# A recurrence filled at a lower pace, two jobs swapped, and two heads' queries copied out of their banks

## The chip, the cores and the metric

The kernel runs on one core of one Trainium2 chip. The metric is the device time of one execution, in microseconds; the time before is the median of three runs. The engines are TensorE (PE), VectorE (DVE), ScalarE (ACT) and GpSimd (POOL); SyncE (SP) issues most of the loads. Each engine works through its instructions in order and waits on semaphores for the others.

## The reference

One layer of a streaming encoder, on 1024 tokens of width 1024 in float32. Two branches read the same normalised input: stick-breaking attention with 8 heads of 64, and an HGRN2 recurrence with 4 heads of 128. Sigmoid gates merge them, an MLP of width 4096 follows.

```python
xn = rmsnorm(x, norm1_g[layer])
u = xn @ w_in[layer]
q_sb, k_sb, v_sb, f_raw, i_hg, q_hg, g_hg, gate_sb, gate_hg = jnp.split(u, c, axis=-1)
o_sb = merge_heads(stick_breaking_attention(q_sb, k_sb, v_sb))      # by blocks of 128 queries
f = lb + (1.0 - lb) * sigmoid(f_raw)
k_hg = (1.0 - lb) * sigmoid(-f_raw)
# S_t = diag(f_t) S_{t-1} + k_t v_t^T ;  o_t = S_t^T q_t
o_hg = hgrn2_chunkwise(silu(q_hg), k_hg, i_hg, log(f))
o_hg = merge_heads(rmsnorm(o_hg, hg_norm_g)) * silu(g_hg)
g_a, g_b = sigmoid(gate_sb + bg[:D]), sigmoid(gate_hg + bg[D:])
merged = g_a * (o_sb @ w_o_sb) + g_b * (o_hg @ w_o_hg)
h = x + merged @ w_out
h = h + square(relu(rmsnorm(h, norm2_g) @ w_ff1)) @ w_ff2
return rmsnorm(h, final_g)
```

## The kernel before, in words

All products are made in float32 precision from three products of a high and a low half: `three` issues hi·hi, hi·lo and lo·hi, each a 128x128 weight tile against 128x512 moving columns. A weight is split into its halves by a cast on ACT and a subtraction on DVE (`hi_lo`, L156 and L161).

The program has these stages: the first norm, transposes and projections; the attention (about 50 to 330 us), in which items of one head and query block go through `scores`, `weights`, `turn` and `values`; the recurrence (about 330 to 583 us), head by head; the gate products (`gates`, tiles gX, gY); the output projection; the MLP.

The attention and the recurrence are chains over PE, ACT, DVE and POOL which would leave PE waiting. So a stream of jobs, `st`, runs beside them: the projections of the attention's later heads (qk), of the recurrence's forget gates (f0 to f3), queries (q0 to q3) and values (i), ten raw products for the gates (raw0 to raw9; raw8 and raw9 are the two sums for the recurrence's output gates; their tiles are pga8 and pga9, pgq8 and pgq9) and the attention's output projection (sb0 to sb3, tiles pys0 to pys7). A step of a job is six products. `Stream.step` starts a job by splitting its weights and, by `prefetch`, splits the weights of the next job and loads those of the one after. In the attention, `st.advance` takes a share of the steps after each item, up to the job `j_att`, which `st.finish(j_att)` completes at the attention's end.

In the recurrence a pass of the loop over h works at two generators in turn: the levels of head h (`hg_levels`: eight levels of shorter and shorter spans; each multiplies k and q by the decay pp on DVE, and PE makes the scores sl or sd from them, copied out under a mask), and the tail of head h−1 (`hg_tail`: pk, the transposes of k; pkv, the products of k and v; the updates of the state on DVE, L1172; pho0 and pho1, the outputs of the two halves; their norm hon over ACT, POOL and DVE; and pot0 and pot1, its transposes). So the last head's tail is alone in the pass h=4. At each yield of either generator `FILL[h]` steps of the stream are owed, and the whole ones are taken, up to a job that is set for each pass:

```python
upto = (j_i, j_raw[1], j_raw[6], j_sb[1], j_sb[2])[h]
...
owed += FILL[h]
st.advance(int(owed), upto)
owed -= int(owed)
```

A side generator, `sum_forms`, makes the sums of the input for the gate products (tiles gs, L1236 and L1239, with their halves gsh and gsl) from the accumulated inputs that four accumulate-DMAs of POOL write into xnl; one step of it goes with each step of an sb job. Its first sum needs the accumulate-DMAs that raw7 issues (`whole_input`).

What PE, DVE and the others execute is fixed when the program is built: a scheduler puts the instructions of each engine into one order, by the order of the code and its own estimates. The edits therefore move more than the lines they touch.

In the stream the job q_h ends with `silu_epilogue`: ACT takes the sigmoid of a PSUM bank (tile pjq), and DVE multiplies the bank by it; the bank is free for another tile after that.

Of the kernel before, what the change touches and what calls it, by code (L numbers as in the profile page):

```python
# [23 lines left out]
KT = D // P  # L24
# [15 lines left out]
def kernel(  # L40
# [19 lines left out]
    nc = tc.nc  # L60
# [14 lines left out]
    def slot(name, dt=F32):  # L75
        return spool.tile([P, 1024], dt, tag="s", name=name)

    def slot_n(name, n, dt=F32):

        if n <= 512:  # L80
            return hpool.tile([P, 512], dt, tag="h", name=name)
        return slot(name, dt)

    def bank(name):
        return psum.tile([P, 512], F32, tag="p", name=name)
# [49 lines left out]
    def load(dst, src):  # L135
        last_load[0] = after(nc.sync.dma_start(dst, src), last_load[0])
# [4 lines left out]
    def lo_now(behind=None):  # L141
        while owed_wlo:
            after(owed_wlo.pop()(), behind)
# [24 lines left out]
    def mul(out, a, b):  # L168
        return nc.vector.tensor_tensor(out=out, in0=a, in1=b, op=ALU.mult)  # L169
# [317 lines left out]
    class Stream:  # L487
# [8 lines left out]
        def add(self, units, body):  # L496
            self.jobs.append((units, body))
            return len(self.jobs)

        def _start(self):  # L500
            lo_now()
            units, body = self.jobs[self.pos]
            for u in units:
                u.split()
            if (self.pos > 0 or self.eager) and not units[-1].late:
                self.prefetch()
            self.gen = body()

# [44 lines left out]
    def three(ps, wh, wl, xh, xl, first, last, goes_on=False):  # L553
        matmul(ps, wh, xh, start=first, stop=False, skip_group_check=goes_on)
        matmul(ps, wh, xl, start=False, stop=False, skip_group_check=goes_on)
        matmul(ps, wl, xh, start=False, stop=last, skip_group_check=goes_on)
# [37 lines left out]
    def wide_unit(name, mat, c0, n):  # L594
        rows = 1024 // n * P
        return Unit(
            name,
            [
                [(0, n, mat[r : r + rows, c0 : c0 + n].rearrange("(k p) c -> p k c", p=P))]
                for r in range(0, D, rows)  # L600
            ],
            wide=True,
        )
# [298 lines left out]
    def hg_slot(h, key, half):  # L902
        if half == 0:
            hg[h, key] = slot(f"{key}{h}")
        return hg[h, key][:, half * 512 : (half + 1) * 512]
# [28 lines left out]
    u_i = wide_unit("wi", W_IN, C_I, HGW)  # L934
# [18 lines left out]
    def silu_epilogue(h, key):  # L953
        def ep(ps, half):
            t = hg_slot(h, key, half)
            nc.scalar.activation(t, ps, AF.Sigmoid)
            mul(t, ps, t)

        return ep

    j_f, j_q = {}, {}

    def f_job(h):
        u = cols_unit(f"wf{h}", [(W_IN, C_F + h * P, P)])
        j_f[h] = proj_jobs([(f"pjf{h}", u, f_epilogue(h))], xn)

    def q_job(h):
        u = cols_unit(f"wq{h}", [(W_IN, C_QH + h * P, P)])
        j_q[h] = proj_jobs([(f"pjq{h}", u, silu_epilogue(h, "q"))], xn)
# [262 lines left out]
    def half(name, dt=F32):  # L1232
        return hpool.tile([P, 512], dt, tag="h", name=name)
# [36 lines left out]
    def gate_bias(which, cb):  # L1270
        return prm[:, BG + which * KT + cb : BG + which * KT + cb + 1]
# [44 lines left out]
    def raw_job(cb):  # L1316
        u = raw_units[cb]

        def steps_of(ps, wt, w0, half_, k0, start):
            wh, wl = u.hl[wt]  # L1320
            for k in range(4):
                c = (w0 + k) * P
                xh, xl = xn.mov(k0 + k, half_)
                three(
                    ps, wh[:, c : c + P], wl[:, c : c + P], xh, xl, start and k == 0, k == 3, True
                )
                if k % 2 == 1:
                    yield

        def body():  # L1330
            p1, p14, g1 = (half(f"{n}_{cb}") for n in ("p1", "p14", "g1"))
            ps, p4 = bank(f"pga{cb}"), bank(f"pgq{cb}")
            if 6 <= cb < KT:
                load_g1(cb - 6)
            if 5 <= cb < KT:
                sb_units[cb - 5].load()
            if 3 <= cb < KT - 1:
                osb[cb - 3] = slot(f"osr{cb}")
                load(osb[cb - 3], od[cb - 3])
            yield from steps_of(ps, 0, 0, 0, 0, True)  # L1340
            hi_behind[0] = nc.scalar.copy(p1, ps)
            nc.scalar.dma_start(pd[cb][:, 0, :], p1)
            u.split_t()
            st.prefetch()
            hi_behind[0] = None
            yield from steps_of(p4, 1, 0, 1, 4, True)
            add(p14, p1, p4)
            if cb == 3 or cb == KT - 1:
                whole_input(1, int(cb == KT - 1))
            nc.gpsimd.dma_start(pd[cb][:, 1, :], p14)  # L1350
            yield from steps_of(ps, 0, 4, 0, 4, False)
            if cb < KT:
                nc.scalar.activation(g1, ps, AF.Sigmoid, bias=gate_bias(0, cb))
            else:
                nc.scalar.activation(g1, ps, AF.Sigmoid)
                mul(g1, ps, g1)
            nc.scalar.dma_start(gd[cb], g1)
            if 4 <= cb < KT:
                a_sb.put(cb - 4, osb.pop(cb - 4))

        return st.add([u], body)
# [3 lines left out]
    def load_g1(cb):  # L1365
        g1r[cb] = half(f"g1r{cb}")
        load(g1r[cb], gd[cb])
# [4 lines left out]
    def whole_input(i, j):  # L1372
        for kp in range(2):
            h, l = (t.bitcast(F32) for t in xn.t[i, 2 * j + kp])
            nc.gpsimd.dma_start(l, h, accum_op=ALU.add)
            whole[i, j, kp] = l
# [82 lines left out]
    f_job(0)  # L1459
    f_job(1)  # L1460
    q_job(1)
    raw_job(KT + 1)
    f_job(2)
    j_att = j_f[2]
    q_job(2)
    j_i = i_job()
    f_job(3)
# [858 lines left out]
        values(*ready.popleft())  # L2326


    FILL = (3.4, 2.2, 2.8, 2.9, 2.9)
    owed = 0.0  # L2330
    for h in range(NHG + 1):
        lev = hg_levels(h) if h < NHG else iter(())
# [3 lines left out]
        while going:  # L2336
            going = False
            for g in (lev, tail):
# [3 lines left out]
                if next(g, StopIteration) is not StopIteration:  # L2342
                    going = True
                    owed += FILL[h]
                    st.advance(int(owed), upto)
# [105 lines left out]
```

## Time and profile before

| what | us |
|---|---|
| median of three runs | 1451.55 (1451.54 to 1451.67) |
| the profiled execution | 1451.45 |
| its span | 1449.7 |
| PE busy | 1429.0 |
| DVE busy | 1118.8 |
| ACT busy | 676.5 |
| POOL busy | 142.5 |

The mean granted clock of TensorE was 0.995. A row of PE's waits reads: the tile that PE wanted to write, the engine and tile that it waited for, and total us, times, longest. A row of the timeline reads: start, duration, engine, line, operation, output and inputs, shape, and in brackets the idle time ahead of it with what ended it. Matmuls are pipelined, so a 128x512 product shows 0.39 us and starts 0.23 us after the one before it. A helper has one line for all its uses (L128 is every product, L161 and L169 most subtractions and multiplications on DVE), so the tile's name tells the place.

### The profile page before, as it was taken

The numbers are of one execution on the slowest core, as the hardware profiler recorded it, in microseconds if no ns is written. First come the engines' busy times: TensorE is split into PE (matmuls) and PEld (weight loads), VectorE is DVE, ScalarE is ACT, GpSimd is POOL, SyncE is SP. The second block draws the span as 40 slices with busy tenths as digits, with TensorE's granted clock in tenths as the row PEclk, the third lists the DMA queues.
The fourth block names the chain that finished last, engine by engine and source line by source line (L and its number), as shares of the span: only waits on it lengthen the run. The fifth ranks groups of instructions, "written<-read, shape, count | busy, mean of one in ns | idle before, by whom it ended". The sixth has DMA issues, their size and how long they took to land.

```text
span 1449.7 us, 19206 instructions
## 1 busy us (share of the span) xinstructions
PE 1429.0 (99%) x7056; PEld 1197.9 (83%) x7056; DVE 1118.8 (77%) x1537; ACT 676.5 (47%) x1173; POOL 142.5 (10%) x338
## 2 busy tenths in 40 slices
PE   9999999999999998999999999999999999999998
PEld 8888888888888887788888888888888888888886
DVE  6579999999568889588877898666666757768765
ACT  6366666673233434333235574444444533423443
POOL 3022222110011031000000200000000000000032
PEclk9999999999999999899999999999999999999999
DMA  7123445453025774355488414444445974676825
GB/s 235 28 66 88 117 101 89 75 108 117 0 61 155 234 202 164 117 166 176 132 293 278 146 59 141 151 159 155 150 160 191 352 262 182 246 277 246 281 101 184
DMA packets 161333, 233.53 MB, mean 161 GB/s; under 512 B 26028, under 2 KB 93144, under 8 KB 161240
## 3 DMA queue, kind: packets, MB, share of 16 engines
q1 hardware_dynamic: 145400, 190.11, 39.1%
q0 software_dynamic: 11520, 34.61, 9.5%
q10 hardware_dynamic: 4320, 7.60, 1.4%
q8 instruction: 55, 0.90, 0.3%
q14 instruction: 38, 0.31, 0.1%
HBM read 167.27 MB, written 65.01 MB: 160 GB/s over the span
## 4 chain that ended last, share of the span: by engine, by line
PE 94%; DVE 3%; ACT 1%; issue 1%; POOL 1%; DMA 0%; ACTq 0%; DVEq 0%; POOLq 0%
PE pm L128 21%; PE pX L128 9%; PE pW L128 6%; PE pY L128 6%; PE pjqk L128 5%; PE gX L128 4%; PE pga L128 4%; PE gY L128 4%; PE pyh L128 3%; PE pys L128 3%; PE pjf L128 3%; PE pjv L128 3%; PE po L128 2%; PE z L128 2%; PE pjq L128 2%; PE pji L128 2%
## 5 line engine op out<-in xcount | busy, mean ns | idle before, releaser
L156 ACT CAST whid<-w 128x1024 fp32r<-128x1024 f32 x30 | 31.6, 1053 | 154.7 <-PE pm L128 86.1
L808 DVE TENSOR_TENSOR_SCAN rm<-rm,bits 128x511 f32<-128x511 f32 (+7 forms) x72 | 87.2, 1218 | 9.0 <-ACT rm L786 8.6
L128 PE MATMUL pm<-wlod,sh 128*128 128x512 f32 x240 | 93.6, 390 | 0.0
L128 PE MATMUL pm<-whid,sl 128*128 128x512 f32 x240 | 93.5, 390 | 0.0
L128 PE MATMUL pm<-whid,sh 128*128 128x512 f32 x240 | 93.5, 389 | 0.0
L128 PE MATMUL pm<-th,sl 128*128 128x512 f32 (+1 forms) x210 | 81.4, 387 | 0.0
L128 PE MATMUL pm<-tl,sh 128*128 128x512 f32 (+1 forms) x210 | 81.4, 387 | 0.0
L128 PE MATMUL pm<-th,sh 128*128 128x512 f32 (+1 forms) x210 | 81.3, 387 | 0.0
L161 DVE TENSOR_TENSOR wlod<-w,whid 128x1024 fp32r<-128x1024 f32 x30 | 36.7, 1223 | 53.3 <-ACT whid L156 53.3
L161 DVE TENSOR_TENSOR sl<-sa,sh 128x1024 fp32r<-128x1024 f32 x56 | 68.3, 1220 | 0.0
L156 ACT CAST wTh<-pw 128x512 fp32r<-128x512 f32 (+2 forms) x96 | 43.4, 485 | 43.1 <-PE pw L131 33.7
L156 ACT CAST sh<-sa 128x1024 fp32r<-128x1024 f32 x56 | 57.2, 1046 | 7.1 <-DMA sa<-ad 7.1
L2087 POOL TENSOR_SCALAR fss<-fss 128x1 f32<-128x1 f32 x8 | 4.5, 561 | 562.1 <-ACT fsc L2082 561.6
L161 DVE TENSOR_TENSOR wTl<-pw,wTh 128x512 fp32r<-128x512 f32 (+2 forms) x96 | 50.2, 546 | 5.6 <-ACT wTh L156 5.3
L128 PEld LDWEIGHTS pm<-wlod,sh 128*128 128x128 f32 x240 | 45.1, 188 | 9.9 <-DVE wlod L161 0.4
L128 PEld LDWEIGHTS pm<-whid,sh 128*128 128x128 f32 x240 | 45.1, 188 | 9.4
L128 PEld LDWEIGHTS pm<-whid,sl 128*128 128x128 f32 x240 | 45.0, 188 | 9.2
L169 DVE TENSOR_TENSOR bt<-bt,rm 128x511 f32<-128x511 f32 (+7 forms) x72 | 49.0, 686 | 3.8
L789 ACT ACTIVATE bt<-z 128x512 f32<-128x512 f32 (+3 forms) x96 | 47.9, 501 | 4.9 <-DMA od<-osb 2.6
L128 PE MATMUL pX<-sql,t1h 128*128 128x512 f32 x128 | 50.1, 391 | 0.1
L128 PE MATMUL pX<-sqh,t1h 128*128 128x512 f32 x128 | 49.9, 390 | 0.0
L128 PE MATMUL pX<-sqh,t1l 128*128 128x512 f32 x128 | 49.9, 390 | 0.0
(931 smaller groups left out, 4473.7 us busy)
## 6 DMA issues: line engine op xcount, KB each, us to landing
w<-in_w_ff_dram SPq DMA_DIRECT2D x72, 512.0 KB, 6.1
sa<-ad SPq DMA_DIRECT2D x56, 512.0 KB, 7.1
ad<-a SPq DMA_DIRECT2D x32, 256.0 KB, 2.2
ad<-s SPq DMA_DIRECT2D x16, 512.0 KB, 5.5
tw<-in_w_out_dram POOLq DMA_DIRECT2D x24, 256.0 KB, 4.1
pr<-pd SPq DMA_DIRECT2D x10, 512.0 KB, 5.1
x<-in_x_dram SPq DMA_DIRECT2D x8, 512.0 KB, 9.7
xnl<-xnh POOLq DMA_DIRECT2D x8, 512.0 KB, 9.4
```

Source lines behind the costliest of these rows:

```text
L128: return pe(nc.tensor.matmul(*a, **k))
L156: hi_last[0] = after(in_turn("act", nc.scalar.copy(dst, src)), hi_behind[0])
L161: nc.vector.tensor_tensor(out=dst, in0=src, in1=hi.bitcast(F32), op=ALU.subtract),
L169: return nc.vector.tensor_tensor(out=out, in0=a, in1=b, op=ALU.mult)
L789: nc.scalar.activation(bt[:, s0 : s0 + e], z[:, :e], AF.Sigmoid, scale=0.125)
L808: sc = nc.vector.tensor_tensor_scan(out=rr, data0=rr, data1=bits[:, 1024 - nk + a : 1024 - nk + b][:, ::-1], initial=rm[:, b : b + 1] if i ...
L2087: nc.gpsimd.tensor_scalar(out=ssq, in0=ssq, scalar1=1.0 / D, scalar2=EPS, op0=ALU.mult, op1=ALU.add)
```

## The change

```diff
@@ class Stream, _start @@
             units, body = self.jobs[self.pos]
             for u in units:
                 u.split()
-            if (self.pos > 0 or self.eager) and not units[-1].late:
+            if (self.pos > 0 or self.eager) and not units[-1].late and units[-1] is not u_i:
                 self.prefetch()
             self.gen = body()
@@ silu_epilogue @@
             t = hg_slot(h, key, half)
             nc.scalar.activation(t, ps, AF.Sigmoid)
+            if h < 2:
+                x = slot_n(f"qx{h}_{half}", 512)
+                nc.scalar.copy(x, ps)
+                ps = x
             mul(t, ps, t)
@@ the stream's jobs @@
     f_job(0)
     f_job(1)
     q_job(1)
-    raw_job(KT + 1)
     f_job(2)
-    j_att = j_f[2]
+    j_att = raw_job(KT + 1)
     q_job(2)
@@ the recurrence @@
-    FILL = (3.4, 2.2, 2.8, 2.9, 2.9)
+    FILL = (3.4, 2.0, 2.6, 2.6, 2.9)
```

There are four edits. The pace of the passes h=1, 2 and 3 is 2.0, 2.6 and 2.6 steps for each yield, where it was 2.2, 2.8 and 2.9. The job raw9 comes behind f2, and is the last that the attention completes. When the job i starts, the weights of the next job, f3, aren't split yet, and those of q3 aren't loaded. For q of heads 0 and 1, ACT copies the bank (two halves each) into an SBUF tile qx, and DVE multiplies from there.

On PE, at the end of the recurrence, before the change. The rows are the last of the second half's output pho of head 3, the two transposes pot, and the first gate product gX.

```order
L128 MATMUL pho_1_5876<-v_3976,sc_5170 128x128
L128 MATMUL pho_1_5876<-k_4436,q_4559 128x128
L131 MATMUL pot_0_5895<-ident,hon_0_5842 128x128 x4
L131 MATMUL pot_1_5901<-ident,hon_1_5878 128x128 x4
L128 MATMUL gX_5907<-gsh_5634,whig_5765 128x512
```

And with the change, from the last of the eighteen fill products (pys4 and pys5) that stand behind pho1:

```order
L128 MATMUL pys_0_5872<-asbh_5483,wo02l_5611 128x512
L131 MATMUL pot_0_5885<-ident,hon_0_5764 128x128 x4
L128 MATMUL pys_1_5893<-asbh_5147,wo02h_5610 128x512
L128 MATMUL pys_1_5893<-asbl_5148,wo02h_5610 128x512
L128 MATMUL pys_1_5893<-asbh_5147,wo02l_5611 128x512
...
L128 MATMUL pys_1_5893<-asbh_5483,wo02l_5611 128x512
L131 MATMUL pot_1_5909<-ident,hon_1_5839 128x128 x4
L128 MATMUL gX_5915<-gsh_5697,whig_5807 128x512
```

Twelve fill products (three are shown, and the last) now stand between the two pots, where nothing stood; likewise eighteen between pho1 and pot0.

On DVE, in the levels of the last head, before. The rows begin with the masked copy of level 3's scores; gs are the first sums of the inputs, g1r is the gate of the sb jobs, and the k and q of 128x32x16 are those of level 5.

```order
L1133 COPY_PREDICATED sc_5170<-masks,sl_3_1_5517 128x512
L169 TENSOR_TENSOR g1r_5348<-pys_0_5505,g1r_5348 128x512
L1236 TENSOR_TENSOR gs_5574<-xnl_539,xnl_571 128x1024
L161 TENSOR_TENSOR wo02l_5560<-wo02r_5350,wo02h_5559 128x1024
L161 TENSOR_TENSOR gsl_5583<-gs_5548,gsh_5582 128x1024
L1133 COPY_PREDICATED sc_5170<-masks,sl_4_0_5586 128x512
L169 TENSOR_TENSOR g1r_5503<-pys_0_5567,g1r_5503 128x512
L169 TENSOR_TENSOR k_4436<-k_4436,pp_4435 128x32x16
L169 TENSOR_TENSOR q_4559<-q_4559,pp_4435 128x32x16
```

And with the change, from the same masked copy:

```order
L1137 COPY_PREDICATED sc_5116<-masks,sl_3_1_5455 128x512
L161 TENSOR_TENSOR wo01l_5494<-wo01r_5273,wo01h_5493 128x1024
L1240 TENSOR_TENSOR gs_5605<-xnl_523,xnl_555 128x1024
L169 TENSOR_TENSOR g1r_5271<-pys_0_5497,g1r_5271 128x512
L1137 COPY_PREDICATED sc_5116<-masks,sl_4_0_5514 128x512
L169 TENSOR_TENSOR k_4462<-k_4462,pp_4461 128x32x16
L169 TENSOR_TENSOR q_4573<-q_4573,pp_4461 128x32x16
```

The first sum gs now stands between the masked copy of level 3 and the k and q of level 5, where the second sum, the weights of the third sb job and a half gsl stood.

On DVE, in the first head's levels, before: the subtractions that split the weights of f3 (wf3l) and of q3 (wq3l), and the k and q of levels 3 (128x128x4) and 4 (128x64x8).

```order
L161 TENSOR_TENSOR wf3l_3917<-wf3r_3778,wf3h_3916 128x1024
L169 TENSOR_TENSOR k_2800<-k_2800,pp_2799 128x128x4
L169 TENSOR_TENSOR q_1747<-q_1747,pp_2799 128x128x4
...
L161 TENSOR_TENSOR wq3l_4365<-wq3r_3920,wq3h_4364 128x1024
L1133 COPY_PREDICATED sc_3801<-masks,sl_2_0_3941 128x512
L1133 COPY_PREDICATED sc_3801<-masks,sl_2_1_3946 128x512
L169 TENSOR_TENSOR k_2800<-k_2800,pp_2799 128x64x8
L169 TENSOR_TENSOR q_1747<-q_1747,pp_2799 128x64x8
```

And with the change:

```order
L169 TENSOR_TENSOR k_2804<-k_2804,pp_2803 128x128x4
L169 TENSOR_TENSOR q_1747<-q_1747,pp_2803 128x128x4
...
L161 TENSOR_TENSOR wf3l_4383<-wf3r_3786,wf3h_4382 128x1024
L1137 COPY_PREDICATED sc_3809<-masks,sl_2_0_3943 128x512
L1137 COPY_PREDICATED sc_3809<-masks,sl_2_1_3948 128x512
L169 TENSOR_TENSOR k_2804<-k_2804,pp_2803 128x64x8
L169 TENSOR_TENSOR q_1747<-q_1747,pp_2803 128x64x8
...
L169 TENSOR_TENSOR q_1747<-q_1747,pp_2803 128x32x16
...
L161 TENSOR_TENSOR wq3l_4389<-wq3r_4386,wq3h_4388 128x1024
```

The split of f3's weights stands one level later, that of q3's behind level 5's k and q.

## The prediction

> **What bounds the kernel now.** I read the page's head first, then PE's waits, then the stretch of the recurrence in windows, then the rows of PE and DVE in it.
>
> ```profile
> span 1449.7 us, 19206 instructions
> PE 1429.0 (99%) x7056; PEld 1197.9 (83%) x7056; DVE 1118.8 (77%) x1537; ACT 676.5 (47%) x1173; POOL 142.5 (10%) x338
> ```
>
> PE is busy for 1429.0 of 1449.7 us, and the change adds and removes no matmul. So only the 20.7 us in which PE stands still, and time in which its clock is low, can be won; anything beyond that can only be lost. PE's waits, with total us, times and longest:
>
> ```profile
> PE pot L131 <- DVE hon L169: 2.5, 1, 2.5
> PE pho L128 <- DVE k L1172: 2.3, 3, 1.2
> PE pk L131 <- DVE k L169: 2.0, 1, 2.0
> PE pga L128 <- DVE q L169: 1.3, 1, 1.3
> PE pw L131 <- DVE bt L169: 1.0, 1, 1.0
> PE sl L128 <- DVE q L169: 0.9, 2, 0.7
> ```
>
> Three of them, 6.8 us, lie at the end of the last head's recurrence, and all have DVE behind them. The windows show how that place differs from what is before it (busy us of PE, PEld, DVE, ACT, POOL, then granted clock, DMA share, GB/s):
>
> ```profile
> 495.00:555.00 60.00, 59.85 (x344) 50.84 (x342) 51.98 (x75) 26.00 (x50) 13.27 (x17) 1.00 0.73 211
> 555.00:574.00 19.00, 16.45 (x101) 14.09 (x101) 18.81 (x26) 10.47 (x22) 1.71 (x4) 1.00 0.33 109
> 574.00:584.00 10.00, 5.57 (x24) 4.43 (x25) 6.79 (x11) 5.00 (x13) 2.09 (x3) 0.69 0.33 109
> ```
>
> From 495 to 555 PE hardly waits and DVE has 8.0 us of 60 to spare; from 555 to 574 DVE has 0.2 of 19 to spare and PE loses 2.5; from 574 to 584 PE loses 4.4 of 10. The fill work was spent too early: it covered levels that had room, and the tail, a chain over DVE, ACT and POOL, stands bare. The rows of PE there, and then the chain of waits:
>
> ```profile
> 555.11 1.12 PE L128 MATMUL sl<-q,k 128*64 128x64 f32 x16 [0.26 <-DVE q L169]
> 558.24 0.98 PE L131 MATMUL pk<-ident,k 128*128 128x128 f32 x7 [2.02 <-DVE k L169]
> ...
> 577.64 0.56 PE L128 MATMUL pho<-v,sc 128*128 128x128 f32 x2
> ...
> 582.36 1.12 PE L131 MATMUL pot<-ident,hon 128*128 128x128 f32 x4 [2.54 <-DVE hon L169]
> 583.13 0.78 PE L128 MATMUL gX<-gsh,whig 128*128 128x512 f32 x1
> 583.70 0.63 PE L128 MATMUL gX<-gsl,whig 128*128 128x512 f32 x1
> ...
> 587.97 0.39 PE L128 MATMUL gX<-gsh,wlog 128*128 128x512 f32 x1
> 588.20 0.39 PE L128 MATMUL gY<-gsh,tgh 128*128 128x512 f32 x1
> ```
>
> ```profile
> 579.07 0.82 ACT hon L1195 x6
> 580.57 1.02 POOL hn_y L257
> ...
> 582.36 1.12 PE pot L131 x4
> 583.48 4.88 PE gX L128 x12
> 588.36 2.75 PE gY L128 x12
> ```
>
> A second loss hides in "busy": gX's 12 products take 588.20 − 583.13 = 5.07 us where gY's twelve take 2.75. The granted clock is halved from about 577.7 (the pho row of 0.56 us where its like take 0.39) to 588.0. That costs 2.3 us in gX and some 0.3 in the last pot: 2.6 us.
>
> The row comes first here: the clock fell though no single idle before it was over 1.2 us; PE was about half busy from 574 to 577.7. [...]
>
> **The change, part by part.**
>
> *Pace 2.2, 2.8, 2.9 to 2.0, 2.6, 2.6 for passes 1, 2 and 3.* By the order of the instructions on PE, the count of fill products ahead of each marker falls by 6 at pass 1, by 12 to 24 through pass 2, by 36 at the second head's last levels, by 48 up to level 5 of the last head, and is back at 0 at gX. Nothing is lost: 48 products of 0.23 us (2.75 for twelve), 11 us, move behind. In the tail there now stand eighteen between sl of level 6 and pk where there was none, twelve between pk and pkv, twelve between pkv and pho, eighteen before the second pho, eighteen before the first pot and twelve between the pots. What goes:
> - pk's 2.02: its k comes three wide DVE operations and a narrow one after level 6's q, 4.1 us by the DVE rows below; PE has sl of level 6 (1.12) and eighteen products (4.1) between, 5.2. Gone, with 1.1 us over.
> - pho's 2.3 (three waits on the state updates): eighteen products, 4.1 us, run ahead of the second pho, while DVE does the updates with wide operations between them. Gone, by walking both queues with 0.75 us over at the first pho and 1.5 at the second.
> - pot's 2.54: thirty products, 6.9 us, between the second pho and the last pot, against the 4.7 us from 577.64 to 582.36 in which ACT, POOL and DVE work today. Gone, even with one more wide operation ahead of hon on DVE.
> - sl's 0.26 is counted below. Sum 6.86 us.
> - With PE full, the half clock goes: 2.6 us. If it stays, that stays.
>
> What is late next: PE comes to the levels of the last head up to 11 us sooner. DVE must keep up there:
>
> ```profile
> 551.41 1.22 DVE L161 TENSOR_TENSOR gsl<-gs,gsh 128x1024 fp32r<-128x1024 f32 x1
> 552.54 1.22 DVE L1239 TENSOR_TENSOR gs<-gs,xnl 128x1024 f32<-128x1024 f32 x1
> 553.68 0.69 DVE L169 TENSOR_TENSOR k<-k,pp 128x512 f32<-128x512 f32 x1
> 554.28 0.69 DVE L169 TENSOR_TENSOR q<-q,pp 128x512 f32<-128x512 f32 x1
> ```
>
> From start to start a 1024-wide operation costs 1.13 us, a 512-wide one 0.60. In the new order, between level 5's q and level 6's q, DVE has four wide ones (gs, gsl, gsl, gs), one masked copy and three narrow ones: 4.52 + 0.62 + 1.8 + 0.1 = 7.06 us. PE has sl of level 5 and twelve products between, 1.14 + 2.75 = 3.9, and walking both orders from the end of head 2's tail on, with these durations, puts PE's arrival at level 5 2.3 us behind its q. 7.06 − 3.9 − 2.3 = 0.9 us: PE waits there, where it waited 0.26. The bounds: 0, if the arrival is 0.9 later, and 2.9, the 11 us asked for less the 8.0 that DVE has to spare. I take 0.9, since it follows the order.
>
> A new queueing stands in that walk: gs of the first sum form now waits on DVE ahead of g1r and of level 5's k and q. It needs an accumulate-DMA of POOL; the page's list of DMA issues gives their median, the rows of the tile their spread:
>
> ```profile
> xnl<-xnh POOLq DMA_DIRECT2D x8, 512.0 KB, 9.4
> ```
>
> ```profile
> DMA to landing us min/median/max: 4.6/9.4/13.1
> ```
>
> With a landing near the median the k and q it holds back are still 2.3 us ahead of PE; at 13.1 PE waits about 0.4. From there each us of landing is a us of PE.
>
> *No prefetch at the start of the i job.* The split of wf3 moves from ahead of level 3's k and q to ahead of level 4's, and that of wq3 from ahead of level 4's to after level 5's.
>
> ```profile
> 349.34 1.27 DVE L161 TENSOR_TENSOR wf3l<-wf3r,wf3h 128x1024 fp32r<-128x1024 f32 x1
> ...
> 354.84 1.26 DVE L161 TENSOR_TENSOR wq3l<-wq3r,wq3h 128x1024 fp32r<-128x1024 f32 x1
> ...
> 358.67 2.02 PE L128 MATMUL sl<-q,k 128*128 128x128 f32 x16 [0.67 <-DVE q L169]
> ```
>
> The second one delayed level 4's pair by 1.13 us, and PE waited 0.67 for it: 0.7 us gone. Both splits stay far ahead of the f3 and q3 jobs, which start after all of this head's levels; were wq3 late, f3's products cover it.
>
> *Four copies by ScalarE for q of heads 0 and 1.* No work is saved:
>
> ```profile
> L169 DVE TENSOR_TENSOR q<-q,pp x36: 683/687/693, 334.5 to 558.1; 128x512 f32<-128x512 f32 x36
> L169 DVE TENSOR_TENSOR q<-pjq,q x8: 667/686/693, 156.6 to 435.6; 128x512 f32<-128x512 f32 x8
> ...
> L1341 ACT COPY p<-pga x10: 581/587/622, 169.9 to 518.2; 128x512 f32<-128x512 f32 x10
> ```
>
> The product costs DVE 0.69 us from the bank or from SBUF, and ACT gains four copies of 0.59. [...] What a copy can win is the bank. The first raw job waits 1.26 us for it:
>
> ```profile
> 162.40 1.48 DVE L808 TENSOR_TENSOR_SCAN rm<-rm,bits 128x639 f32<-128x639 f32 x1
> 164.01 0.83 DVE L169 TENSOR_TENSOR bt<-bt,rm 128x639 f32<-128x639 f32 x1
> 164.75 0.69 DVE L169 TENSOR_TENSOR q<-pjq,q 128x512 f32<-128x512 f32 x1
> ```
>
> But the new order puts that 1.48 us scan ahead of the bt that the next pw transposes, and pga behind a wTl on DVE. So pga would still start near 165.5, the wait now standing before pw. Value 0; ends a gain of 1.3 and a loss of 0.6, one copy in line. ACT is 47% busy and hides the rest.
>
> *The tenth raw job behind f2.* It swaps two jobs within the attention. Its add on DVE now comes near the last pair's bt, on which pw waits 0.96 (in the list above); on SP one load of wf2 passes those of the tenth raw job, on POOL one store of p comes later. Nobody reads these for hundreds of us. Value 0, ends ±0.6, one narrow DVE operation.
>
> Sum: −6.86 − 2.6 − 0.67 − 0.26 + 0.9 = −9.5. The profiled execution took 1451.45 us, 0.1 under the median, so 1442.0 us. Some 0.2%, 2.9 us, is what a measurement here can tell from no change.
>
> **The rivals.**
>
> *The waits move in part.* DVE's reserve of 8.0 us is not usable at the levels that need it: DVE must follow PE within one level. Then 2.9 us of waits appear in the last head, and a half-empty stretch brings the low clock back for one spell of the price seen, 2.6. Gain 9.5 − 2.0 − 2.6 = 4.9: 1446.5. For it speaks DVE's 99% from 555 to 574; against it that DVE idled 8.0 us before 555. [...]
>
> *Nothing comes of it*, since the tail is bound by DVE alone: its end would stay at 582.3 whatever PE does, PE only waiting earlier. 1451.5, give or take 2. Against it, DVE itself stands still for 2.3 us here, for a chain that begins with PE's pho:
>
> ```profile
> 581.61 0.69 DVE L169 TENSOR_TENSOR hon<-pho,hn_y 128x512 f32<-128x512 f32 x1 [2.29 <-POOL hn_y L257]
> ```
>
> *Slower.* The bare levels drop the clock where PE is dense. All 6.9 us of waits reappear in passes 2 and 3, and the clock falls at two of these places for the 10.2 us it was low here, in the midst of 512-wide products, which lose half of it, 5.1 each. The old spell's 2.6 and the 0.67 are gone: 1451.45 − 2.6 − 0.67 + 10.2 = 1458.4. It decides from the second such place on; one alone gives 1453.3. Against it: with 99% of DVE's time taken from 555 to 574 and 2.5 us of waits, the clock stayed at 1.00.
>
> **How the numbers follow.** My forecast (1439.8 to 1445) has 0.62, waits that move in part (1445 to 1448.6) 0.21, nothing 0.07, slower 0.10. The low end is 1442.0 less the 0.9 and the 1.3; the high end, 1447.5, leaves out the last two and a little of the second. Faster 0.83, same 0.07, slower 0.10.
>
> **What would show it.** Right: no PE wait of pk, pho or pot over 0.3 us, a clock of 1.00 through gX, gX's twelve in 2.75, no sl wait in the first head, one sl wait near 1 us in the last. Wrong: sl or pk waits on DVE k or q of over 2 us in heads 1 to 3; a clock under 1 before the tail; pga or pw near 165 waiting over 2 us; DVE's gs waiting for a DMA.

## The result, and the profile after

With the change the kernel takes 1438.17 us (median of five runs, 1437.93 to 1438.95), against 1451.67 for the kernel before in the same comparison: a ratio of 0.9905, with a 95% interval from 0.989 to 0.9919. It is faster by 13.5 us where 9.5 was forecast, and 1.6 us under the low end of the range. The direction and the mechanism held; two prices were too low, and one wait that was forecast didn't come.

The head of the page after, and PE's waits in it:

```profile
span 1436.2 us, 19231 instructions
PE 1423.2 (99%) x7056; PEld 1193.2 (83%) x7056; DVE 1118.6 (78%) x1537; ACT 678.0 (47%) x1177; POOL 146.6 (10%) x338
```

```profile
PE warm L128 <- POOL ident masks.py:199: 2.2, 1, 2.2
PE pw L131 <- DVE bt L169: 2.2, 2, 1.2
PE xnt L131 <- DVE x L631: 0.4, 1, 0.4
PE pjqk L128 <- DVE xnl L339: 0.3, 1, 0.3
```

No wait of pot, pho, pk or sl is left. The two waits of pw lie in the attention; the other rows are the program's start. PE's idle time fell from 20.7 to 13.0 us, which is 7.7; the other 5.8 us came out of PE's *busy* time, from 1429.0 to 1423.2, although the matmuls are the same 7056. That second number is where most of the error lies: the prediction had 2.6 of it.

The stretch of the recurrence's end in windows (the columns as before):

```profile
495.00:545.00 50.00, 50.00 (x308) 42.79 (x308) 46.79 (x69) 22.25 (x45) 13.72 (x15) 1.00 0.78 211
545.00:575.00 30.00, 30.00 (x162) 25.63 (x162) 25.09 (x37) 14.97 (x34) 6.20 (x8) 1.00 0.50 174
```

PE is full throughout and the clock stays at 1.00; DVE, 99% busy in the tail before, has 4.9 of 30 us to spare. The chain of waits there is PE alone:

```profile
564.48 4.10 PE pys L128 x18
568.58 0.44 PE pot L131 x4
569.02 2.77 PE pys L128 x12
571.79 0.44 PE pot L131 x4
572.23 2.75 PE gX L128 x12
574.98 2.72 PE gY L128 x12
```

gX's twelve products take 2.75 us, as gY's do, where they took 4.88 in this view before.

### The profile page after: what moved, and what is told of

It reads as the page before. It is cut to its first block, busy times and chain, and to the rows that moved or that the text cites. A ratio compares the mean times of both kernels' runs of the same rounds, so it can differ in the third digit from the quotient of the medians.

```text
span 1436.2 us, 19231 instructions
## 1 busy us (share of the span) xinstructions
PE 1423.2 (99%) x7056; PEld 1193.2 (83%) x7056; DVE 1118.6 (78%) x1537; ACT 678.0 (47%) x1177; POOL 146.6 (10%) x338
## 4 chain that ended last, share of the span: by engine, by line
PE 76%; DVE 0%; POOL 0%; ACT 0%; issue 0%
PE pm L128 21%; PE pX L128 9%; PE pW L128 6%; PE pY L128 6%; PE gX L128 4%; PE gY L128 4%; PE pys L128 3%; PE pga L128 3%; PE pji L128 3%; PE pyh L128 3%; PE sl L128 3%; PE pwX L128 2%; PE pjq L128 2%; PE pgq L128 2%; PE pwY L128 2%; PE pwW L128 2%
```

## The experiments

The two spans differ by 13.5 us, and 13.4 of them lie behind PE's first product. To see where, I added up, for each tile, the distance from the start of each product to the start of the next, and kept the idle time apart. Idle time gone: pot 2.54, pho 2.31, pk 2.02, sl 0.26 in the tail; 0.80 in the first head; 0.28 net at the attention's end; against that, PE idles some 0.4 longer at the program's start. Busy time gone: gX 2.24, pho 1.38, pot 1.12, some 0.2 each in pw and pys. The runs below ask which edit and which cause each belongs to. All times before in them lie between 1451.0 and 1454.1; each comparison was made on one chip.

### The lower pace alone

```diff
 # the kernel before
-    FILL = (3.4, 2.2, 2.8, 2.9, 2.9)
+    FILL = (3.4, 2.0, 2.6, 2.6, 2.9)
```

> Before, with the three lower paces alone. Theory A (the waits cost more than their idle time shows): the tail's idle time, 7.1 us, goes; with it the drain and refill of PE around each of six waits, about 0.27 us each by the pitch of the products beside them, 1.2 to 1.6 in all; and the half clock, which by pitches cost 2.24 us in gX and 1.5 in pho and pot, 3.7 in all. Gain 12.2 us, so about 1439.4. Rival B (the prediction's prices were right and the rest of the gain comes from the other three edits): gain of 6.9 + 2.6 + 0.3 = 9.8 less a new wait of 0 to 0.9, so 1441.8 to 1442.7.

Measured: 1439.96 us against 1451.75, ratio 0.9916 (0.9901 to 0.9931). That is 11.8 us from the pace, 0.4 less than theory A said and 2 to 3 more than B. In its trace gX, pho, pot and the tail's waits change by the same amounts as in the full change, to 0.01 us, and the first head's waits stay:

```profile
PE pga L128 <- DVE q L169: 1.2, 1, 1.2
PE pw L131 <- DVE bt L169: 1.0, 1, 1.0
PE sl L128 <- DVE q L169: 0.8, 2, 0.7
```

### Everything but the pace

```diff
 # the changed kernel
-    FILL = (3.4, 2.0, 2.6, 2.6, 2.9)
+    FILL = (3.4, 2.2, 2.8, 2.9, 2.9)
```

> The change without the lower paces: no prefetch at the i job, the copies of q, and the swap of raw9 and f2. Theory A: the first head's two waits of 0.80 us go with 0.3 of drain, and 0.3 at the attention's end; 1.1 to 1.4 us, so about 1450.3, the tail as before with its 7.1 us of waits and gX at half clock. Rival B: these three carry some 4 us, 1447.6.

Measured: 1450.92 against 1451.75, ratio 0.9989 (0.998 to 0.9999). By products and waits its trace is 1.8 us shorter than before's: 0.80 idle and 0.22 busy in the first head, 0.28 and 0.22 at the attention's end, some 0.3 in stages that the edits don't touch. The tail's waits are there again. The median shows 0.8 us of this, since the times of both kernels fall into two groups (see the last section); the lower groups, 1449.2 to 1449.8 and 1451.0 to 1451.8, are some 1.8 to 1.9 apart. Theory A; B's 4 us are excluded.

### The tail kept busy without being filled

Why did the busy time fall? In the kernel before I put products of the identity, which compute nothing that is used, where PE stood idle in the last head's tail. The products that are used still wait for DVE; only the emptiness goes.

```diff
 # the kernel before, hg_tail
+        dm = None
...
+            if h == NHG - 1 and half == 1:
+                dm = bank("dm")
...
             for j in range(4):
                 c = 4 * half + j
...
+                if dm is not None and c > 4:
+                    for _ in range((4, 10, 6)[c - 5]):
+                        matmul(dm[:, 0:P], ident, ident, start=True, stop=True)
                 if c:
                     matmul(po[:, js], qh[:, cs], Ss[:, cs], start=False, stop=True)
...
             pot = bank(f"pot{h}_{half}")
+            if dm is not None and half == 1:
+                for _ in range(20):
+                    matmul(pot[:, 0:P], ident, ident, start=True, stop=True)
```

> Before, with 40 extra 128x128 products of the identity in the last head's tail (4, 10 and 6 ahead of the three waits of pho1, and 20 ahead of the last pot), where PE stands idle. They compute nothing that is used. The waits on DVE stay. Theory A: the clock fell because PE was half empty from 574 to 582; kept busy, it stays at 1.00, gX takes 2.75 us, and 3.7 us are won: about 1447.9. Rival C: the clock fell for another reason, or only the waits themselves count: gX still at half clock, 1451.6 or a little over.

Measured: 1452.29 against 1451.75, ratio 1.0 (0.9991 to 1.001). The time is rival C's, but the trace shows that it isn't C's reason. The granted clock is 1.00 from 574 to 592, over gX too, and the extra products cost what that gives: each of these float32 products of 128 columns appears as two passes, so the 40 of them make 80 (x8, x4, x16, x12 and x40) and take 9 us. The last pot starts at 586.77 us where it was 582.36.

```profile
582.31 4.63 PE L128 MATMUL pot<-ident 128*128 128x128 f32 x40
586.77 0.60 PE L131 MATMUL pot<-ident,hon 128*128 128x128 f32 x4
587.13 0.47 PE L128 MATMUL gX<-gsh,whig 128*128 128x512 f32 x1
```

So it was repeated with half of them:

```diff
-                    for _ in range((4, 10, 6)[c - 5]):
+                    for _ in range((2, 5, 3)[c - 5]):
...
-                for _ in range(20):
+                for _ in range(10):
```

> The warmed tail again with half as many extra products (2, 5, 3 and 10): in the run before each showed as two passes, so that they took 9 us where 6 stood idle and pushed the tail back. They compute nothing that is used. Theory A: the waits on DVE stay as long as before, the clock stays at 1.00 through gX, and what the half clock cost (2.24 us in gX, 1.5 in pho and pot) is won, less a low window at pk's wait if one falls there (1 us): 1447.9 to 1449. Rival C (the clock costs nothing of its own, the tail's end is set by DVE): 1451.6.

Measured: 1448.87 against 1452.66, ratio 0.9978 (0.9967 to 0.9989): 1.6 to 4.8 us faster by doing 20 useless products. Within either of the two groups of times that the last section tells of, the gain is some 3 us. In the trace the last pot even starts later, at 583.50 us where it was 582.36; 1.6 us of that is a new spell of low clock, shown below. Windows, and rows of PE:

```profile
555.00:574.00 19.00, 16.98 (x97) 14.46 (x98) 17.45 (x25) 9.16 (x15) 1.08 (x2) 0.91 0.31 96
574.00:584.00 10.00, 8.57 (x69) 7.86 (x68) 7.07 (x13) 5.76 (x19) 2.73 (x4) 1.00 0.39 133
584.00:592.00 8.00, 8.00 (x38) 6.61 (x37) 4.99 (x7) 0.69 (x1) 0.00 (x0) 1.00 0.57 164
```

```profile
558.11 0.98 PE L131 MATMUL pk<-ident,k 128*128 128x128 f32 x7 [2.02 <-DVE k L169]
558.85 0.61 PE L128 MATMUL pys<-asbh,wo02h 128*128 128x512 f32 x1
...
561.82 0.63 PE L128 MATMUL pys<-asbl,wo02h 128*128 128x512 f32 x1
...
562.58 0.39 PE L128 MATMUL pys<-asbh,wo02h 128*128 128x512 f32 x1
...
583.50 0.66 PE L131 MATMUL pot<-ident,hon 128*128 128x128 f32 x4 [0.72 <-DVE hon L169]
583.91 0.47 PE L128 MATMUL gX<-gsh,whig 128*128 128x512 f32 x1
```

The half clock from 574 on is gone (1.00 and 1.00, where it was 0.69 and 0.75), with gX 2.24 us shorter. That it isn't a chance of one trace shows in the mean granted clock: 0.997 to 0.999 in all eight executions, 0.994 to 0.996 in all eleven of the kernel before. PE was busy for 8.57 us from 574 to 584, where it was 5.57: in this tail the emptiness brought the low clock, and it has a price beside the waits. And a new spell shows: after pk's 2.02 us, the same wait as before, the products run 0.43 us apart, where others run 0.23 apart, from about 559.0 to 562.4, one spell of 3.4 us, which cost 1.6 us in pys. The trace of the run with 40 products has the same spell behind the same wait (a granted clock of 0.91 from 555 to 574, as here). In the trace of the kernel before, the clock was 1.00 from 555 to 574, over the same wait; the last section has the traces side by side.

### A pace lower still

```diff
 # the changed kernel
-    FILL = (3.4, 2.0, 2.6, 2.6, 2.9)
+    FILL = (3.4, 2.0, 2.4, 2.4, 2.9)
```

> The change with paces 2.0, 2.4, 2.4 for passes 1 to 3, in place of 2.0, 2.6, 2.6. In the change's trace level 6's q is 1.1 us ahead of PE and pk's k 2.2 us. Theory A (little margin is left and DVE can't come sooner): some 24 products, 5 us, fewer stand ahead of level 6, and 3 to 5 us of waits on DVE's k or q appear in the last head; with the drains 1441 to 1443. Rival D (DVE follows, since it waits for PE itself): no wait over 0.5 us, 1438.2.

Measured: 1439.59, ratio 0.9913 (0.9898 to 0.9927), 1.4 us over the change. The one wait that appears stands where both theories looked, but is smaller than A's:

```profile
538.28 1.15 PE L128 MATMUL sl<-q,k 128*64 128x64 f32 x16 [1.34 <-DVE q L169]
```

DVE follows for most of the 5 us that PE is earlier, not for all. This is the prediction's new wait at level 6, one step of the pace further on.

### The copies of q left out, or half of them

```diff
 # the changed kernel, silu_epilogue: first run
-            if h < 2:
-                x = slot_n(f"qx{h}_{half}", 512)
-                nc.scalar.copy(x, ps)
-                ps = x
 # second run
-            if h < 2:
+            if half == 1 and h < 2:
```

> The change without the four copies of q. Theory A (the copies only move a wait): pw's 1.2 us near 164 goes and pga's 1.2 near 165 comes back; 1438.2, give or take 0.3. Rival F (the copies free the bank and win it): 1439.4.

> The change with copies for the second halves of q0 and q1 alone. DVE's order near 162 is then that of before (bt ahead of the 639-wide scan), and no multiplication from the bank stands ahead of pga. Theory A: no wait of pw near 164; pga waits on wTl until about 165.0, so 0.3 to 0.5 us less than with the change, 1437.8. Rival: pw's wait stays, 1438.2.

Measured: 1438.17 without copies, ratio 0.9902 (0.9887 to 0.9917), and 1438.12 with half of them, 0.9901 (0.9886 to 0.9916). The copies are worth nothing. The waits of the two, in that order:

```profile
PE pga L128 <- DVE q L169: 1.3, 1, 1.3
PE pw L131 <- DVE bt L169: 0.9, 1, 0.9
```

```profile
PE pga L128 <- DVE wTl L161: 1.3, 1, 1.3
PE pw L131 <- DVE bt L169: 0.9, 1, 0.9
```

With all copies pw waits 1.2 us near 164; without them pga waits 1.3 near 165 for q's bank; with half of them pga waits the same 1.3 us, for wTl, a low half of the attention's transposed weights. Theory A was right on the first and missed the second: no part of the wait went, since wTl ends about as late on DVE as the multiplication did. In all three runs it is DVE that PE waits for there.

### The prefetch kept, and the swap undone

```diff
 # the changed kernel, _start: first run
-            if (self.pos > 0 or self.eager) and not units[-1].late and units[-1] is not u_i:
+            if (self.pos > 0 or self.eager) and not units[-1].late:
 # second run
+    raw_job(KT + 1)
     f_job(2)
-    j_att = raw_job(KT + 1)
+    j_att = j_f[2]
```

> The change with the prefetch at the start of the i job as before. Theory A: the first head's two waits come back, 0.80 us and some 0.2 to 0.3 of drain, 1439.2; the tail unchanged. Rival G (with the new pace DVE has the split done early enough): 1438.2.

> The change with raw9 ahead of f2 again. Theory A: the short wait of po at the attention's end (0.26 us, with its drain 0.5) comes back, 1438.7. Rival (the swap is worth nothing): 1438.2.

Measured: 1439.19 with the prefetch, ratio 0.9908 (0.9894 to 0.9923), and 1438.6 without the swap, 0.9904 (0.9886 to 0.9922): 1.0 and 0.4 us over the change, as theory A has both. The waits that come back, in that order:

```profile
PE sl L128 <- DVE q L169: 0.6, 1, 0.6
```

```profile
PE po L128 <- ACT wTh L156: 0.3, 1, 0.3
```

The intervals of these two ratios overlap that of the change; it is the waits in the traces, and their size, that carry the reading.

### Another job behind q0

```diff
 # the changed kernel
         if h == 4:
-            q_job(0)
             raw_job(KT)
+            q_job(0)
 # second run: this, and the copies of q left out as above
```

> A try for a faster kernel: the change with raw8 ahead of q0 in the stream, so that another job follows q0 where pw waits 1.2 us near 164. If the wait belongs to that place alone, 1436.8; if it only moves to the job that then follows, 1438.2.

> The same without the copies of q: if the bank of q0's second half holds up whatever job follows, a wait near 1.2 us stays and the time is 1438.2; if not, 1436.8.

Measured: 1438.87, ratio 0.9906 (0.989 to 0.9921), and 1438.97 without copies, 0.9906 (0.9891 to 0.9921). The wait near 164 goes, and two others of 1.0 us take its place (those of the first run):

```profile
PE z L128 <- DVE osb L887: 1.0, 1, 1.0
PE pgq L128 <- DVE QL L161: 1.0, 1, 1.0
```

No kernel that I tried is faster than the changed one by more than 0.05 us.

## Why the prediction was right and wrong

**The tail's waits: right.** 7.12 us of idle time (2.02, 2.3, 2.54, 0.26) were named, and 7.13 went. None came back in the heads before. That is the larger part of the forecast, and its mechanism held: the run with the pace alone loses the same waits.

**The half clock: right in kind, too small.** The sum has "2.3 us in gX and some 0.3 in the last pot". gX gave 2.24. But the clock was low over the last of pho's products and both pots as well. Two windows of before, cut where the clock changes, show where that begins:

```profile
574.30:577.72 3.42, 1.56 (x11) 1.18 (x11) 2.80 (x5) 0.62 (x1) 0.59 (x1) 1.00 0.20 77
577.72:581.13 3.41, 2.10 (x9) 1.44 (x8) 1.61 (x4) 2.06 (x10) 0.75 (x2) 0.50 0.73 235
```

By the distances of its products, pho lost 0.7 us and the two pots 0.8 to it. The whole is 3.7 us where 2.6 stood: 1.1 missed. That the low clock would go with PE full was an estimate; after, the window 545 to 575 has PE busy for 30.00 of 30 us, at 1.00.

**The price of a wait: the step that failed.** The prediction starts from "only the 20.7 us in which PE stands still, and time in which its clock is low, can be won", and each wait entered the sum with the idle time in brackets. There was a third thing to win, inside PE's busy time, which the sum put at nothing. PE's rows of before and after show it; each row is one product in two passes:

```profile
574.36 0.39 PE L128 MATMUL pho<-v,sc 128*128 128x128 f32 x2
575.92 0.49 PE L128 MATMUL pho<-k,q 128*128 128x128 f32 x2 [1.18 <-DVE k L1172]
576.25 0.39 PE L128 MATMUL pho<-v,sc 128*128 128x128 f32 x2
```

```profile
562.98 0.39 PE L128 MATMUL pho<-v,sc 128*128 128x128 f32 x2
563.20 0.39 PE L128 MATMUL pho<-k,q 128*128 128x128 f32 x2
563.42 0.39 PE L128 MATMUL pho<-v,sc 128*128 128x128 f32 x2
```

From the first of the three rows to the last are 1.89 us before and 0.44 after: the wait cost 1.45 us and shows 1.18. The pass ahead of the wait is counted as busy until its own end, 0.27 us after its start, while in the rows after the next one starts after 0.11: call it the drain. And the row behind the wait shows 0.49 us, 0.10 more than the others: the refill. That is 0.27 us for this wait, and the same for pho's two others; pot's comes close to it, and those of sl and pk show 0.05 to 0.2. The tail's six waits held some 1.3 us of this, and the first head's two 0.2. The sum had none of it. These are readings of rows; no run removed the drains and kept the waits.

**The new wait of 0.9 at level 6: wrong.** In the trace after, DVE's rows at levels 5 and 6, and then PE's:

```profile
530.65 1.22 DVE L1240 TENSOR_TENSOR gs<-xnl,xnl 128x1024 f32<-128x1024 f32 x1 [0.86 <-DMA xnl<-xnh]
...
533.61 0.68 DVE L169 TENSOR_TENSOR q<-q,pp 128x512 f32<-128x512 f32 x1
...
537.26 1.23 DVE L161 TENSOR_TENSOR gsl<-gs,gsh 128x1024 fp32r<-128x1024 f32 x1 [1.10 <-ACT gsh L156]
...
541.88 0.69 DVE L169 TENSOR_TENSOR q<-q,pp 128x512 f32<-128x512 f32 x1
```

```profile
539.63 1.20 PE L128 MATMUL sl<-q,k 128*32 128x32 f32 x32
543.71 1.15 PE L128 MATMUL sl<-q,k 128*64 128x64 f32 x16
```

From q to q DVE took 8.3 us, 1.2 more than the 7.06 that the walk had, since it waits 1.1 for ACT. PE took 4.1, where the walk had 3.9. But level 5's q was ready 5.3 us ahead of PE where the walk put 2.3, and so level 6's was 1.1 ahead. The larger error was in the walk's start, carried over two heads; that the wait didn't come was no merit of the walk, which had DVE too fast. DVE's gs did wait for the accumulate-DMA, 0.86 us, which the prediction names both as a new queueing and as a sign of being wrong; it cost PE nothing. (By the prediction's own figures the longest landing, 13.1 us against a median of 9.4 and with 2.3 in hand, would cost PE 1.4 us, not 0.4.)

**The first head: right, a little small.** 0.67 was summed; the two waits hold 0.80 and their drain 0.2, 1.0 us in all; the run with the prefetch kept loses that 1.0.

**The copies: right.** Value 0, a pw wait of 1.2 in place of pga's 1.26, and the run without copies takes the same time, 1438.17 us: the copy brought nothing.

**raw9 behind f2: taken as 0 within ±0.6, worth 0.4.** What it won is the wait of po for ACT's wTh at the attention's end, 0.26 us, with its drain, which the prediction didn't look at; that it fell inside the bounds is luck.

Against the sum of 9.5 that makes 1.1 of half clock, 1.5 of drains, 0.9 of a wait that didn't come, 0.1 in the first head and 0.4 from the swap: 13.5, for 13.4 between the traces. Differences of some 0.2 either way in stages that the change doesn't touch, such as the start, are not explained.

**The rivals.** Waits that move in part did not occur at this pace; one step lower they begin, with one of 1.34 us. The half clock did not move into the dense levels: its granted clock is 1.00 in each window of the recurrence after. Nothing of the kind that would have made it slower showed. The range's low end allowed for the wait of 0.9 not coming and for 1.3 from the copies, but held no bound for the price of a wait that is certain.

## What to carry to other kernels

Count a stall of PE from the start of the product ahead of it to the start of the product behind, and take off what the same rows measure in a dense place: idle time in brackets leaves out the drain and the refill, here up to 0.27 us for each wait. Where the granted clock is low, go through all rows under it, not only the largest group; and add up how much PE works just ahead of it, not only the longest wait: here two waits of pho, 1.18 and 0.68 us, left 1.56 us of work in 3.42, and the clock was 0.50 behind them (next section). Fill work that a stream hands out belongs where the wait ends last; here 48 products taken from levels with room and put into an empty tail brought 12 of the 13.5 us, and one step further the levels began to wait.

## What the runs showed of the hardware

In the kernel before, the granted clock fell to 0.50 with no single idle time over 1.18 us in the 3.42 us ahead, and stayed there for 10.2 us (577.72 to 587.95). In the two runs with extra products the low spell was 3.4 us, a third of that. The traces are read here in windows of this length, counted from where the clock changed in the same trace. Three pairs of neighbouring windows, from everything but the pace, from 40 products and from 20, and a fourth from the kernel before (the columns as before; the first busy time is PE's, and the clock is the third number from the end):

```profile
552.53:555.95 3.42, 1.75 (x19) 1.20 (x17) 3.25 (x6) 2.90 (x4) 0.00 (x0) 1.00 0.00 0
555.95:559.36 3.41, 2.79 (x16) 2.45 (x17) 3.41 (x5) 1.05 (x1) 0.00 (x0) 1.00 0.20 77
```

```profile
554.58:557.99 3.41, 1.63 (x19) 1.09 (x17) 3.24 (x6) 2.78 (x4) 0.00 (x0) 1.00 0.01 2
557.99:561.40 3.41, 2.90 (x11) 2.62 (x12) 3.41 (x7) 1.04 (x1) 0.00 (x0) 0.50 0.20 77
```

```profile
555.63:559.04 3.41, 1.39 (x16) 1.25 (x15) 3.41 (x7) 2.38 (x4) 0.00 (x0) 1.00 0.20 77
559.04:562.45 3.41, 3.41 (x10) 2.63 (x9) 3.41 (x5) 1.16 (x3) 0.00 (x0) 0.50 0.00 0
```

```profile
553.82:557.24 3.42, 2.14 (x21) 1.51 (x19) 3.25 (x5) 3.18 (x5) 0.00 (x0) 1.00 0.02 7
557.24:560.65 3.41, 2.41 (x14) 2.14 (x15) 3.41 (x6) 1.13 (x2) 0.00 (x0) 1.00 0.20 77
```

PE was busy for 1.75 us in the first of these windows in everything but the pace and for 2.14 in the kernel before, and the clock of the next was 1.00. It was busy for 1.63 us with 40 products and for 1.39 with 20, and the clock of the next was 0.50, as it was behind the 1.56 us from 574.30 to 577.72 in the kernel before. pk's wait of 2.02 us lies whole in the window 555.63 to 559.04 of the run with 20 products, where the spell followed; with 40 products 557.99 divides it into 1.51 and 0.51, and the spell followed too; in the trace of the kernel before, where none did, 557.24 divides it into 1.02 and 1.00. The rest of the long spell in the kernel before, and the window behind it:

```profile
581.13:584.54 3.41, 2.18 (x7) 1.92 (x8) 2.93 (x3) 2.22 (x3) 0.45 (x1) 0.50 0.00 1
584.54:587.95 3.41, 3.41 (x9) 2.65 (x8) 0.03 (x1) 0.00 (x0) 0.00 (x0) 0.50 0.87 250
587.95:591.36 3.41, 3.41 (x16) 2.82 (x15) 1.51 (x3) 0.00 (x0) 0.00 (x0) 1.00 0.39 133
```

In this spell the windows with 2.10 and 2.18 us of PE were followed by 0.50 again; behind the 3.41 here, and behind 3.41 with 20 products and 2.90 with 40, the products run 0.23 us apart again. What sets the clock beyond these places was not shown.

The kernel before seems to pay for one more such spell in some executions: the spans of the 36 in the comparisons with the experiments lie at 1449.2 to 1450.2 us (18, mean clock 0.995 or 0.996) and at 1450.8 to 1452.3 (18, mostly 0.994). The two are some 1.6 us apart, which is what one such spell cost. That it is pk's wait there too is inferred, as no execution of the upper group was traced; the changed kernel, without that wait, has spans of 1436.2 to 1436.5 alone.
